# First layer of a two-layer trunk: products moved from GpSimd to VectorE, ScalarE and a load, gate weights folded in bulk, heads in another order

## The chip, the cores and the metric

One core of one Trainium2 chip runs the whole program in one launch. The metric is the device time of an execution in microseconds, here the median of three. Lower is better. Engines are named as in the profile: PE is TensorE, DVE is VectorE, ACT is ScalarE, POOL is GpSimd, SP is SyncE, which only issues transfers.

## The reference

The input x has 256 tokens of 1024 channels. The first layer is an mLSTM block, the second an attention block of three branches. The change touches the first layer alone, so here is what it computes:

```python
h = rmsnorm(x, ml_norm)
x_in, z = split(h @ w_in)                      # 2048 channels each
conv = sum(x_pad[:, tap:tap + S] * conv_w[tap] for tap in range(4))
x_conv = silu(conv + conv_b)
q, k = headwise(x_conv, w_q), headwise(x_conv, w_k)    # 4x4 blocks: 512 of them
v = headwise(x_in, w_v)
gates = concat([q, k, v]) @ w_if + b_if                # 8 gate rows, 4 heads
hh = mlstm(q * DH ** -0.5, k, v, i_pre, log_sigmoid(f_pre))
x = x + ((layernorm(hh) * ln_w + skip * x_conv) * silu(z)) @ w_out
```

## The kernel before, in words

Every large product is done in three: each weight is rounded to a high part and the remainder kept as a low part, the activations likewise, and high by high, low by high and high by low are summed. Weights come in units of 1 MB, each in two halves (load_unit, L258). SP loads a half into a raw buffer (L273; four of them, so two units), ACT rounds it (L274), and the remainder is made either by DVE (L280) or by ACT and a transfer that POOL issues and that adds in place (L277, L278). The units 0, 1, 2 and 11 have both remainders on DVE, most others have the second one by transfer.

The first layer begins with loads of x transposed, in four pieces, between the pieces of the unit 0. ACT and DVE make the high and low parts of x (L342, L343). The squares for the norm (L351 to L356) are two on POOL and two on ACT, their sums two on POOL and one on DVE. norm1 (L384) makes one row of 256 factors, rb1, with two small products on PE and a power on POOL (L325). It is called in the middle of the first evacuation.

A loop over four heads (L431) follows. Each head takes two units of the projection (project_channels, L402), and DVE multiplies each result by rb1 into the tile xin (L438, two buffers). In the first pass, after the first unit, SP is given the constants cst, the gate weights wif and x by tokens (L441 to L449), each kept back by a small DVE copy of a column of rb1. Then the head's products are prepared: POOL spreads the 4x4 blocks of two weights into block-diagonal tiles m (blockdiag, L396, with the mask bm out of cst), bdq for the query and key together, bdv for the value. DVE folds the gate weights of that head (gate_weights, L461, for bdv and for q). The convolution has four taps. The first is on ACT (L476), the others on DVE (L487, 44 in all), except that head 0 has its second tap on ACT (L480) and the sum on POOL (L482). ACT takes the SiLU of the whole head (L489). PE then makes q (L497), v (L504) and the scores (L511, L512). The tiles gva and gsc gather the gate columns (L508 on POOL, L516 on DVE).

After the heads, the value is split in high and low parts (split_v, L529): the low part is on POOL for the heads 0 and 2, on DVE for the heads 1 and 3. The gate chain, a second loop over heads (L591), eight units of z (L653) and the output projection (L694) follow. POOL multiplies x_conv by the skip weight, once per head (L641).

The program order is not the order on the engines. When the program is built, a planner walks through it in a simulation of time and puts each engine's instructions into a fixed order. An earlier line goes first where both could start, and a later line that is ready earlier may overtake. So the L641 products run among the heads, and the load of pkb, written at L724, is issued at the start. Each engine and each queue then keeps to its order: an instruction that waits holds all behind it.

Of the kernel before, what the change touches and what calls it, by code (L numbers as in the profile page):

```python
# [9 lines left out]
F32 = mybir.dt.float32  # L10
# [18 lines left out]
V_POOL = (0, 2)  # L29
# [106 lines left out]
def prep(x, ml_norm, ml_w_in, ml_conv_w, ml_conv_b, ml_w_q, ml_w_k, ml_w_v, ml_w_if, ml_b_if,  # L136
# [30 lines left out]
    wif = np.repeat(ml_w_if[0].reshape(3, 16, 32, 1, 4, 8), 4, 3).transpose(0, 2, 3, 1, 4, 5).reshape(3, P, 16, 4, 8)  # L167
    o["wif"] = np.concatenate([np.stack([wif[0], wif[1]], 2).reshape(P, 1024), wif[2].reshape(P, 512)], 1)
# [34 lines left out]
def trunk(ctx, tc, a, out, dbg=None):  # L203
# [80 lines left out]
    plan = [(a["wi1"], i, KT, 256) for i in range(16)] + [(a["wo1"], i, 4, 512) for i in range(8)]  # L284
# [44 lines left out]
    nc.sync.dma_start(pka, a["pka"])  # L329
# [54 lines left out]
    def norm1():  # L384
# [11 lines left out]
    def blockdiag(src, dt, n=P):  # L396
        t = T([P, 4, n], dt, tag="m2", bufs=M2)
# [33 lines left out]
    for h in range(NH):  # L431
        xin = T([P, 4, S + 3], tag="xin", bufs=2)
        GP.memset(xin[:, :, 0:3], 0.0)
        for u in range(2):
            def evac_x(ps, x_=xin[:, 2 * u:2 * u + 2, 3:], first=(h, u) == (0, 0)):
                if first:
                    norm1()
                V.tensor_tensor(x_, ps, spread(rb1), op=OP.mult)  # L438
            project_channels(a["wi1"], 2 * h + u, evac_x, ("px", "px", "acc1")[(2 * h + u) % 3])
            if (h, u) == (0, 0):  # L440
                V.tensor_copy(cst[:, 0:1], rb1[:, 0:1])  # L441
                nc.sync.dma_start(cst, a["cst"][:, 0:n_res])
                wifs = [T([P, 16, n // 128, 8], tag="zt", bufs=ZT, name="wif") for n in (1024, 512)]
                for t, o_, n in zip(wifs, (0, 1024), (1024, 512)):
                    V.tensor_copy(t[:, 0, 0, 0:1], rb1[:, 0:1])
                    nc.sync.dma_start(t.rearrange("p a b c -> p (a b c)"), a["wif"][:, o_:o_ + n])
                for i in range(2):
                    V.tensor_copy(xt[i][:, 0, 0:1], rb1[:, 0:1])
                    nc.sync.dma_start(xt[i], a["x"][:, i * 512:(i + 1) * 512].rearrange("(t p) c -> p t c", p=P))  # L449
# [694 lines left out]
```

## Time and profile before

| what | value |
|---|---|
| median of three runs | 377.86 us (377.17 to 378.06) |
| the profiled execution | 378.87 us |
| its span, first to last instruction | 377.1 us |
| mean granted TensorE clock | 0.984 |
| busy: PE, DVE, ACT, POOL | 350.6, 255.7, 241.5, 134.7 us |

The span is what the views of the trace are laid out on. The profiled execution is 1.77 us longer than its span, and 1.01 us longer than the median. A matmul's end is modelled, so a busy PE says that it had an instruction and not how fast it went; the granted clock says how fast.

### The profile page before, as it was taken

The page shows a single profiled execution, that of the slowest core. Times are in us where ns is not written, and L with a number is a line of the kernel's source. Part 1 is how long each engine was busy: PE and PEld are TensorE (multiplying, and loading weights), DVE is VectorE, ACT ScalarE, POOL GpSimd, SP SyncE. Part 2 cuts the span into 40 slices and gives each one's busy share as a digit, 9 for nine tenths or more (in the row PEclk, how much of TensorE's full clock was granted, in tenths as well). Part 3 has the DMA queues.
Part 4 walks back from the last instruction along what each step waited for, and adds up shares of the span by engine and source line. Part 5 has one row for each costly group of instructions (what it writes and reads, how often), then busy time and mean ns, then how long its engine had stood idle before and what let it go on. Part 6 is the DMA issues. An engine that isn't in the chain of part 4 may idle for free.

```text
span 377.1 us, 6621 instructions
## 1 busy us (share of the span) xinstructions
PE 350.6 (93%) x2399; PEld 313.8 (83%) x2399; DVE 255.7 (68%) x535; ACT 241.5 (64%) x438; POOL 134.7 (36%) x165
## 2 busy tenths in 40 slices
PE   6998799979999979999999799999879999999991
PEld 6998799869998968988887699999869996777771
DVE  5976999756476548983243736687979789684515
ACT  6674669738468649765653744372579789996304
POOL 5226377433301124610100303283430283857003
PEclk9999899999999999999999999999989999999997
DMA  7889758765646978999998897546577865020003
GB/s 260 280 269 315 209 129 217 188 152 125 167 157 159 197 210 217 228 233 296 239 262 239 266 343 216 173 104 155 154 195 209 246 237 158 2 56 2 2 0 112
DMA packets 21633, 69.57 MB, mean 185 GB/s; under 512 B 2528, under 2 KB 2912, under 8 KB 21600
## 3 DMA queue, kind: packets, MB, share of 16 engines
q1 hardware_dynamic: 15472, 48.71, 38.7%
q0 software_dynamic: 4752, 16.83, 24.6%
q10 hardware_dynamic: 1376, 3.61, 2.9%
q8 instruction: 19, 0.31, 0.3%
q14 instruction: 14, 0.11, 0.1%
HBM read 50.87 MB, written 1.05 MB: 138 GB/s over the span
## 4 chain that ended last, share of the span: by engine, by line
PE 39%; DMA 23%; DVE 18%; issue 8%; ACT 8%; POOL 1%; SPq 1%; ACTq 0%; POOLq 0%; DVEq 0%
PE ps L411 17%; DMA wl<-wr 7%; DMA wr<-in_wo_dram 6%; DVE xc L487 6%; PE ps L694 6%; DVE wl L280 4%; DMA wr<-in_wi2z_dram 3%; DMA wr<-in_wi2k_dram 2%; ACT wh L274 2%; PE ps L984 2%; PE ps L909 2%; PE ps L897 2%; DMA cst<-in_cst_dram 2%; DMA xch<-in_xt_dram 1%; ACT wl L277 1%
## 5 line engine op out<-in xcount | busy, mean ns | idle before, releaser
L411 PE MATMUL ps<-hT,wh 128*128 128x256 f32 x832 | 139.5, 293 | 2.4 <-DVE hT L343 1.3
L274 ACT ACTIVATE wh<-wr 128x1024 fp32r<-128x1024 f32 (+2 forms) x90 | 89.5, 1000 | 58.1 <-PE ps L411 21.5
L411 PEld LDWEIGHTS ps<-hT,wh 128*128 128x128 f32 x832 | 121.8, 198 | 4.6 <-DVE hT L343 1.9
L280 DVE TENSOR_TENSOR wl<-wr,wh 128x1024 fp32r<-128x1024 f32 (+2 forms) x57 | 70.9, 1244 | 36.0 <-ACT wh L274 33.2
L411 PE MATMUL ps<-hT,wl 128*128 128x256 f32 x416 | 87.7, 287 | 0.0
L411 PEld LDWEIGHTS ps<-hT,wl 128*128 128x128 f32 x416 | 66.4, 193 | 1.0 <-issue 0.6
L278 POOL DMA_DIRECT2D wl<-wr x33 | 28.7, 877 | 107.9 <-ACT wl L277 103.5
L277 ACT ACTIVATE wl<-wr 128x1024 fp32r<-128x1024 f32 (+1 forms) x33 | 33.8, 1025 | 13.4 <-PE ps L694 6.6
L694 PE MATMUL ps<-wh,r 128*128 128x512 f32 x128 | 41.4, 398 | 0.0
L487 DVE SCALAR_TENSOR_TENSOR xc<-xin,pka,xc 128x256 f32<-128x256 f32 x44 | 30.8, 754 | 0.1
L694 PEld LDWEIGHTS ps<-wh,r 128*128 128x128 f32 x128 | 24.0, 188 | 5.5
L694 PE MATMUL ps<-wl,r 128*128 128x512 f32 x64 | 25.3, 395 | 0.0
L694 PE MATMUL ps<-wh,y 128*128 128x512 f32 x64 | 21.8, 406 | 0.0
L803 POOL TENSOR_TENSOR swap<-swap,trig 128x512 f32<-128x512 f32 x6 | 10.2, 1697 | 18.9 <-DMA swap<-qu 7.3
L775 PE MATMUL ps<-wl,hT 128*128 128x280 f32 (+1 forms) x48 | 15.8, 330 | 1.2 <-DMA wl<-wr 1.2
L846 PE MATMUL ps<-ka,qt 128*128 128x256 f32 (+1 forms) x32 | 12.0, 380 | 3.8 <-DVE nm L852 3.7
L774 PE MATMUL ps<-wh,hT 128*128 128x280 f32 (+1 forms) x48 | 15.5, 329 | 0.0
L776 PE MATMUL ps<-wh,hT 128*128 128x280 f32 (+1 forms) x48 | 15.2, 325 | 0.0
L694 PEld LDWEIGHTS ps<-wh,y 128*128 128x128 f32 x64 | 11.8, 188 | 3.1 <-issue 0.8
L694 PEld LDWEIGHTS ps<-wl,r 128*128 128x128 f32 x64 | 12.0, 188 | 2.8 <-DMA wl<-wr 0.2
L641 POOL TENSOR_TENSOR xc<-xc,pka 128x1024 f32<-128x1024 f32 x4 | 9.8, 2455 | 12.2 <-PE ps L512 12.2
L504 PE MATMUL ps<-m,xin 128*128 128x136 f32 x64 | 9.7, 299 | 3.6 <-DVE m L464 3.5
(473 smaller groups left out, 676.0 us busy)
## 6 DMA issues: line engine op xcount, KB each, us to landing
wr<-in_wi_dram SPq DMA_DIRECT2D x34, 512.0 KB
wl<-wr POOLq DMA_DIRECT2D x31, 512.0 KB, 5.9
wr<-in_wo_dram SPq DMA_DIRECT2D x24, 512.0 KB
wr<-in_wi2k_dram SPq DMA_DIRECT2D x12, 512.0 KB
wr<-in_wi2z_dram SPq DMA_DIRECT2D x8, 512.0 KB
wr<-in_wi2v_dram SPq DMA_DIRECT2D x8, 280.0 KB
cw<-in_cw_dram ACTq DMA_DIRECT2D x4, 512.0 KB
xch<-in_xt_dram SPq DMA_DIRECT2D x4, 256.0 KB
```

The lines of the kernel that those rows point to most:

```text
L274: A.activation(hi[:, k, :], raw[:, k, :], AF.Copy)
L277: A.activation(lo[:, k, :], raw[:, k, :], AF.Copy, scale=-1.0)
L278: GP.dma_start(out=lo[:, k, :].rearrange("p k n -> p (k n)"), in_=raw[:, k, :].rearrange("p k n -> p (k n)"), accum_op=OP.add)
L280: V.tensor_tensor(lo[:, k, :], raw[:, k, :], f32(hi[:, k, :]), op=OP.subtract)
L411: PE.matmul(ps[:, c, :], w, (hl if i == 1 else hh)[:, k, :], start=(k, c, i) == (0, 0, 0), stop=(k, i) == (KT - 1, 2), skip_group_check=True)
L487: V.scalar_tensor_tensor(xc[:, c, :], xin[:, c, tap:tap + S], tap_w(tap, c), xc[:, c, :], op0=OP.mult, op1=OP.add)
L694: PE.matmul(acc, l, r[:, k % 2, cols], start=first and i == 0, stop=last and i == 2)
L774: PE.matmul(o_, lh, hi[:, k % 2, :], start=kt == 0, stop=False)
L775: PE.matmul(o_, lh, lo[:, k % 2, :], start=False, stop=False)
L776: PE.matmul(o_, ll, hi[:, k % 2, :], start=False, stop=kt == KT - 1)
L803: (GP, V)[RE[1]].tensor_tensor(sw, sw, turn(1), op=OP.mult)
L846: PE.matmul(o_, lq, ka[:, g, :, 0:w_], start=True, stop=False)
```

## The change

The squares are all on ACT and their sums on DVE. The high and low parts of x come ahead of the squares in program order, norm1 ahead of the projection, and the second unit's load behind norm1 (N0 is 1). The block-diagonal tiles of the value are loaded with their zeros (wvbd, 1.05 MB: 16 x 128 columns of 128 rows; in two loads, four columns of blocks and twelve). Those of the query are made on DVE. The gate weights of all heads are folded at once, those for the value ahead of head 0's convolution and those for the query behind it; POOL copies a head's part into q. Head 0's convolution becomes like the others'. The SiLU is taken by half a head. DVE takes the low parts of the values and the gva sums; two conversions (ident_r, maskt_r) go from DVE to POOL, and the halved factors rb1h from DVE to ACT. cst, wif and the first part of wvbd are kept back by a column of the squares instead of rb1, x by tokens and pkb by head 2's xin. The program order of projections (A) and products (B) of the heads becomes A0 A1 B0 A2 B1 A3 B2 B3.

```diff
-V_POOL = (0, 2)
-N0 = 2
-CA_ = (1, 2, 3)
-CB_ = (0,)
-CH = 1
+N0 = 1
 SQA = (2, 3)
-SQP = (1, 2)
+SQP = ()
+XTH = 2
+STAGES = "A0 A1 B0 A2 B1 A3 B2 B3"
...
+    o["wvbd"] = np.zeros((32, 4, 16, 32, 4), f)
+    o["wvbd"][np.arange(32), :, :, np.arange(32), :] = own(ml_w_v).reshape(32, 4, 16, 4)
+    o["wvbd"] = o["wvbd"].reshape(P, 16, P)
...
     ahead(N0)
-    nc.sync.dma_start(pka, a["pka"])
...
+    scaled(range(KT), lambda kt: xch0[kt // 4][:, kt % 4, :], gain1)
     sq1 = T([P, 4, S], tag="zt", bufs=ZT, name="sq1")
     for q in range(4):
...
-        (A.activation(o_, x_, AF.Square) if q in SQA else GP.tensor_tensor(o_, x_, x_, op=OP.mult))
+        A.activation(o_, x_, AF.Square)
         if q:
             (GP if q in SQP else V).tensor_tensor(sq1[:, 0:2, :], sq1[:, 0:2, :], o_, op=OP.add)
-    scaled(range(KT), lambda kt: xch0[kt // 4][:, kt % 4, :], gain1)
...
-        V.tensor_scalar(rb1h, rb1, 0.5, None, op0=OP.mult)
+        A.activation(rb1h, rb1, AF.Copy, scale=0.5)
+
+    norm1()
+    ahead(2)
+    nc.sync.dma_start(pka, a["pka"])
...
-        GP.tensor_tensor(t[:, :, 0:P].rearrange("p c (n j) -> p c n j", j=4),
-                         src[:, :, None, :].to_broadcast([P, 4, 32, 4]), bm, op=OP.mult)
+        V.tensor_tensor(t.rearrange("p c (n j) -> p c n j", j=4),
+                        src[:, :, None, :].to_broadcast([P, 4, 32, 4]), bm, op=OP.mult)
...
+    def heads_x(h):
+        xin = xins[h] = T([P, 4, S + 3], tag="xin", bufs=2)
+        GP.memset(xin[:, :, 0:3], 0.0)
+        for u in range(2):
+            def evac_x(ps, x_=xin[:, 2 * u:2 * u + 2, 3:]):
+                V.tensor_tensor(x_, ps, spread(rb1), op=OP.mult)
+            project_channels(a["wi1"], 2 * h + u, evac_x, ("px", "px", "acc1")[(2 * h + u) % 3])
+            if (h, u) == (0, 0):
+                small_weights()
+        if h == XTH:
+            V.tensor_copy(pkb[:, 0:1], xin[:, 0, 3:4])
+            nc.sync.dma_start(pkb, a["pkb"])
+            for i in range(2):
+                V.tensor_copy(xt[i][:, 0, 0:1], xin[:, 0, 3:4])
+                nc.sync.dma_start(xt[i], ...)
...
+    def small_weights():
+        bdvs = folded["bdv"] = T([P, 16, PG], name="bdv")
+        wifs = [T([P, 16, n // 128, 8], tag="zt", bufs=ZT, name="wif") for n in (1024, 512)]
+        V.tensor_copy(cst[:, 0:1], sq1[:, 0, 0:1])
+        nc.sync.dma_start(cst, a["cst"][:, 0:n_res])
+        for t, o_, n in list(zip(wifs, (0, 1024), (1024, 512)))[::-1]:
+            V.tensor_copy(t[:, 0, 0, 0:1], sq1[:, 0, 0:1])
+            nc.sync.dma_start(t.rearrange("p a b c -> p (a b c)"), a["wif"][:, o_:o_ + n])
+        for c, dep in ((slice(0, 4), sq1[:, 0, 0:1]), (slice(4, 16), rb1[:, 0:1])):
+            V.tensor_copy(bdvs[:, c.start, 0:1], dep)
+            nc.sync.dma_start(bdvs[:, c, 0:P], a["wvbd"][:, c, :])
...
+        def gate_weights(out, wgt, wif, nq):
+            tmp = T([P, 16, nq * 4, 8], tag="f4", bufs=F4, name="wtmp")
+            V.tensor_tensor(tmp, wif, wgt[:, :, :, None].to_broadcast([P, 16, nq * 4, 8]), op=OP.mult)
+            V.tensor_reduce(out, tmp.rearrange("p c i g -> p c g i"), axis=AX.X, op=OP.add)
+
+        gate_weights(folded["bdv"][:, :, P:PG], wv, wifs[1], 1)
+        gq = T([P, 16, 8], name="gwq")
+        folded.update(AT=AT, gq=gq, fold_q=lambda: gate_weights(gq, wqk, wifs[0], 2))
...
+            A.activation(xc[:, c, :], xin[:, c, 0:S], AF.Identity, scale=tap_w(0, c), bias=cbias)
         for c in range(4):
-            for tap in range(2 if h in CB_ else 1, 4):
+            for tap in range(1, 4):
                 V.scalar_tensor_tensor(xc[:, c, :], xin[:, c, tap:tap + S], tap_w(tap, c),
                                        xc[:, c, :], op0=OP.mult, op1=OP.add)
-        A.activation(xc, xc, AF.Silu)
+            if c % 2:
+                A.activation(xc[:, c - 1:c + 1, :], xc[:, c - 1:c + 1, :], AF.Silu)
+        if h == 0:
+            folded["fold_q"]()
...
-        gate_weights(q[:, :, S:SG], wqk, wifs[0], 2)
+        GP.tensor_copy(q[:, :, S:SG], folded["gq"][:, own, :])
...
-        GP.tensor_tensor(gva, gva, v[:, :, :, P:PG], op=OP.add)
+        V.tensor_tensor(gva, gva, v[:, :, :, P:PG], op=OP.add)
...
-    V.tensor_copy(ident_r, ident)
+    GP.tensor_copy(ident_r, ident)
-    V.tensor_copy(maskt_r, C("maskt")[:, None, :].to_broadcast([P, 2, P]))
+    GP.tensor_copy(maskt_r, C("maskt")[:, None, :].to_broadcast([P, 2, P]))
...
-        (GP if h in V_POOL else V).tensor_tensor(lo, src, f32(hi), op=OP.subtract)
+        V.tensor_tensor(lo, src, f32(hi), op=OP.subtract)
```

## Rows read from the trace of the kernel before

**Rows 1.** The page's busy times of the engines (busy us, share of the span, instructions).

```profile
PE 350.6 (93%) x2399; PEld 313.8 (83%) x2399; DVE 255.7 (68%) x535; ACT 241.5 (64%) x438; POOL 134.7 (36%) x165
```

**Rows 2.** Busy time of each engine in five stretches of the span: from:to in us, length, then busy us and instructions of PE, PEld, DVE, ACT and POOL, the granted TensorE clock, the share of the 16 DMA engines and GB/s.

```profile
11.80:36.50 24.70, 24.65 (x197) 24.45 (x197) 19.08 (x33) 15.04 (x20) 8.34 (x7) 1.00 0.87 277
36.50:40.90 4.40, 0.93 (x8) 0.96 (x9) 4.40 (x6) 0.00 (x0) 3.58 (x4) 1.00 0.58 216
40.90:44.40 3.50, 3.50 (x19) 3.50 (x19) 3.50 (x8) 3.24 (x6) 1.04 (x1) 0.53 1.02 219
...
77.00:79.50 2.50, 0.13 (x2) 0.00 (x0) 2.50 (x5) 0.00 (x0) 1.31 (x1) 1.00 0.98 211
...
139.50:200.00 60.50, 58.23 (x306) 49.09 (x307) 36.88 (x74) 42.71 (x55) 17.29 (x24) 1.00 0.94 241
```

**Rows 3.** What TensorE waited for in the first 160 us: waiting line, what released it, us in total, times, longest.

```profile
PE ps L504 <- DVE m L464: 3.5, 1, 3.5
PE ps L497 <- DVE gsc L516: 2.4, 1, 2.4
...
PE ps L411 <- DVE hT L343: 1.3, 2, 0.9
```

**Rows 4.** VectorE in order of time ahead of the first wait: start, us, line, operation, tiles and shapes, count, and in brackets the idle time before it with what ended it.

```profile
32.04 0.29 DVE L524 CAST maskt_r<-cst 128x256 fp32r<-128x256 f32 x1 [2.26 <-DMA cst<-in_cst_dram]
32.25 4.83 DVE L487 SCALAR_TENSOR_TENSOR xc<-xin,pka,xc 128x256 f32<-128x256 f32 x4
37.00 2.53 DVE L463 TENSOR_TENSOR wtmp<-wif,pka 128x128 f32<-128x128 f32 x2
```

**Rows 5.** GpSimd in the same time, the first and the last of its six tensor operations in a row from 32.15 to 39.26, with the columns of the group above.

```profile
32.15 1.09 POOL L398 TENSOR_TENSOR m<-AT,cst 128x512 f32<-128x512 f32 x1 [2.95 <-DMA cst<-in_cst_dram]
...
37.95 1.31 POOL L482 TENSOR_TENSOR xc<-xc,x 128x512 f32<-128x512 f32 x1
```

**Rows 6.** The chain of waits: start, us and what held the chain.

```profile
25.97 6.04 DMA cst<-in_cst_dram
```

**Rows 7.** VectorE around the second wait: one operation by itself; then, from other times with no GpSimd tensor operation beside them, six taps in a row and one remainder of a half unit.

```profile
73.40 5.20 DVE L487 SCALAR_TENSOR_TENSOR xc<-xin,pka,xc 128x256 f32<-128x256 f32 x1
...
60.53 2.45 DVE L487 SCALAR_TENSOR_TENSOR xc<-xin,pka,xc 128x256 f32<-128x256 f32 x6
...
26.70 1.22 DVE L280 TENSOR_TENSOR wl<-wr,wh 128x1024 fp32r<-128x1024 f32 x1
```

**Rows 8.** GpSimd at the time of that long operation.

```profile
73.78 2.20 POOL L641 TENSOR_TENSOR xc<-xc,pka 128x1024 f32<-128x1024 f32 x1
75.64 2.66 POOL L534 TENSOR_TENSOR vsp<-v,vsp 128x1024 fp32r<-128x1024 f32 x1
```

**Rows 9.** VectorE while the first unit starts, without and with GpSimd at work beside it.

```profile
5.61 0.87 DVE L343 SCALAR_TENSOR_TENSOR hT<-xch,pk,hT 128x256 fp32r<-128x256 f32 x2
6.41 1.52 DVE L280 TENSOR_TENSOR wl<-wr,wh 128x512 fp32r<-128x512 f32 x1
7.85 1.89 DVE L343 SCALAR_TENSOR_TENSOR hT<-xch,pk,hT 128x256 fp32r<-128x256 f32 x2
9.67 0.68 DVE L280 TENSOR_TENSOR wl<-wr,wh 128x512 fp32r<-128x512 f32 x1
```

**Rows 10.** GpSimd in that time, the last of the four operations on the squares.

```profile
9.81 1.69 POOL L356 TENSOR_TENSOR sq<-sq 128x512 f32<-128x512 f32 x1 [0.74 <-ACT sq L354]
```

**Rows 11.** VectorE from 20 to 105 us grouped by line and shape: line, operation, tiles, shapes, count | busy us, mean ns | idle before.

```profile
L438 DVE TENSOR_TENSOR xin<-ps,rb 128x512 f32<-128x512 f32 x8 | 5.5, 685 | 8.2 <-PE ps L411 8.2
...
L463 DVE TENSOR_TENSOR wtmp<-wif,pka 128x256 f32<-128x256 f32 x4 | 2.7, 680 | 0.0
L464 DVE TENSOR_REDUCE q<-wtmp 128x32 f32<-128x256 f32 x4 | 2.5, 628 | 0.0
L463 DVE TENSOR_TENSOR wtmp<-wif,pka 128x128 f32<-128x128 f32 x4 | 2.0, 495 | 0.0
L464 DVE TENSOR_REDUCE m<-wtmp 128x32 f32<-128x128 f32 x4 | 1.5, 372 | 0.0
```

**Rows 12.** GpSimd from 20 to 105 us, grouped in the same way.

```profile
L641 POOL TENSOR_TENSOR xc<-xc,pka 128x1024 f32<-128x1024 f32 x4 | 9.8, 2455 | 12.2 <-PE ps L512 12.2
...
L534 POOL TENSOR_TENSOR vsp<-v,vsp 128x1024 fp32r<-128x1024 f32 x2 | 6.0, 3010 | 0.0
L398 POOL TENSOR_TENSOR m<-pka,cst 128x512 f32<-128x512 f32 x4 | 4.8, 1210 | 2.9 <-DVE m L464 2.9
```

**Rows 13.** TensorE in order of time: the starts of two units one after the other.

```profile
28.88 2.32 PE L411 MATMUL ps<-hT,wh 128*128 128x256 f32 x18
...
34.64 1.84 PE L411 MATMUL ps<-hT,wh 128*128 128x256 f32 x14
```

**Rows 14.** ScalarE in order of time: the rounding of halves of the units 2 and 4, which needs their loads.

```profile
17.92 1.06 ACT L274 ACTIVATE wh<-wr 128x1024 fp32r<-128x1024 f32 x1 [1.66 <-DVE wl L280]
...
27.72 1.04 ACT L274 ACTIVATE wh<-wr 128x1024 fp32r<-128x1024 f32 x1
```

**Rows 15.** The DMA queues in the first 10 us (packets, MB, share of 16 engines): ScalarE's queue then carries only a load in rows of 544 bytes.

```profile
q10 hardware_dynamic: 144, 0.07, 2.9%
```

**Rows 16.** The chain of waits after the layer's heads: start, us, what held the chain.

```profile
167.58 5.79 DMA wl<-wr
...
173.43 3.77 DMA wr<-in_wo_dram
```

More of the change, by code (lines that the diff above doesn't have):

```diff
@@ L430, in trunk @@
     convw = CA("convw").rearrange("p (t c) -> p t c", t=4)
-    for h in range(NH):
-        xin = T([P, 4, S + 3], tag="xin", bufs=2)
+    xins, zt_ = {}, {}
+    def heads_x(h):
+        xin = xins[h] = T([P, 4, S + 3], tag="xin", bufs=2)
         GP.memset(xin[:, :, 0:3], 0.0)
         for u in range(2):
-            def evac_x(ps, x_=xin[:, 2 * u:2 * u + 2, 3:], first=(h, u) == (0, 0)):
-                if first:
-                    norm1()
+            def evac_x(ps, x_=xin[:, 2 * u:2 * u + 2, 3:]):
                 V.tensor_tensor(x_, ps, spread(rb1), op=OP.mult)
@@ L440, in trunk @@
             if (h, u) == (0, 0):
[L441 to L449, printed above, removed]
@@ new lines, in fold @@
+    def fold():
+        wifs = folded["wif"]
+        wqk = CA("wqk").rearrange("p (c i) -> p c i", c=16)
+        wv = CA("wv").rearrange("p (c i) -> p c i", c=16)
+        atmp = T([P, 16, 4, 4], tag="f4", bufs=F4, name="atmp")
+        V.tensor_tensor(atmp, CA("wkrep").rearrange("p (c i j) -> p c i j", c=16, i=4),
+                        wqk[:, :, 0:4, None].to_broadcast([P, 16, 4, 4]), op=OP.mult)
+        AT = T([P, 16, 4], name="AT")
+        V.tensor_reduce(AT, atmp.rearrange("p c i j -> p c j i"), axis=AX.X, op=OP.add)
+        def gate_weights(out, wgt, wif, nq):
[5 more added lines that the diff above has]
+        folded.update(AT=AT, gq=gq, fold_q=lambda: gate_weights(gq, wqk, wifs[0], 2))
@@ L469, in trunk, with heads_products @@
+    def heads_products(h):
+        if h == 0:
+            fold()
+        xin = xins.pop(h)
+        own = slice(4 * h, 4 * h + 4)
+        bdq = blockdiag(folded["AT"][:, own, :])
+        bdv = folded["bdv"][:, own, :]
         xc = T([P, 4, S], tag="f4", bufs=F4, name="xc")
         tap_w = lambda tap, c: convw[:, tap, 4 * h + c:4 * h + c + 1]
-        if h in CB_:
-            x1 = T([P, 4, S], tag=XT, bufs={"zt": ZT, "sc2": 1}[XT], name="x1")
         for c in range(4):
             cbias = CA("convb")[:, 4 * h + c:4 * h + c + 1]
-            if h in CA_ or h in CB_:
-                A.activation(xc[:, c, :], xin[:, c, 0:S], AF.Identity, scale=tap_w(0, c), bias=cbias)
-            else:
-                V.tensor_scalar(xc[:, c, :], xin[:, c, 0:S], tap_w(0, c), cbias, op0=OP.mult, op1=OP.add)
-            if h in CB_:
-                A.activation(x1[:, c, :], xin[:, c, 1:1 + S], AF.Copy, scale=tap_w(1, c))
-                if CH and c % 2:
-                    GP.tensor_tensor(xc[:, c - 1:c + 1, :], xc[:, c - 1:c + 1, :], x1[:, c - 1:c + 1, :], op=OP.add)
@@ L519, in trunk, with silu_z1, evac_z @@
         scs.append(sc)
+    def silu_z1(h):
+        z = zt_[h] = T([P, 4, S], name="z")
+        for u in range(2):
+            def evac_z(ps, z=z[:, 2 * u:2 * u + 2, :]):
+                V.tensor_tensor(z, ps, spread(rb1), op=OP.mult)
+                A.activation(z, z, AF.Silu)
+            project_channels(a["wi1"], 8 + 2 * h + u, evac_z)
+    for stage in STAGES.split():
+        {"A": heads_x, "B": heads_products, "Z": silu_z1}[stage[0]](int(stage[1]))
     ident_r = TS([P, P], F32R, name="ident_r")
-    V.tensor_copy(ident_r, ident)
+    GP.tensor_copy(ident_r, ident)
     maskt_r = T([P, 2, P], F32R, name="maskt_r")
-    V.tensor_copy(maskt_r, C("maskt")[:, None, :].to_broadcast([P, 2, P]))
+    GP.tensor_copy(maskt_r, C("maskt")[:, None, :].to_broadcast([P, 2, P]))
     causal = C("mask2")
@@ L646, in trunk @@
     for h in range(NH):
-        z = T([P, 4, S], tag="zt", bufs=ZT, name="z")
-        for u in range(2):
+        z = zt_[h] if h in zt_ else T([P, 4, S], tag="zt", bufs=ZT, name="z")
+        for u in range(0 if h in zt_ else 2):
             def evac_z(ps, z=z[:, 2 * u:2 * u + 2, :]):
@@ L722, in after_block @@
         squares(ss2, n, tb)
-    nc.sync.dma_start(pkb, a["pkb"])
     gain2 = CB("g")
```

26 lines of the change are left out of this document (7 added, 19 removed).

## The prediction

> **What bounds the kernel now.** I read the busy times first, then a table by stretch, then TensorE's waits, then the queues of the engine that each wait names. TensorE is busy for 350.6 of 377.1 us [rows 1], so a change is worth what it takes out of TensorE's idle time or of its time at the lower clock. In the stretch 11.8 to 36.5 it is full: 24.65 of 24.70 us at a granted clock of 1.00 [rows 2]. Then come 4.40 us with only 0.93 us of work, and 3.50 us at 0.53, which is the lower level of 1.2 GHz; it fell after the idle time [rows 2]. The wait is for the gate columns of the value's block-diagonal tile, DVE's L464, 3.5 us [rows 3]. A second hole is at 77.0 to 79.5, 2.4 us for gsc [rows 2, 3].
>
> Both waits name DVE, and both come from POOL beside it. Six taps in a row take 2.45 us, 0.41 each, with no tensor operation on POOL [rows 7]; four ahead of the first wait take 4.83, 1.2 each, and two small products 2.53 [rows 4], while POOL works without a pause [rows 5]. In the second case one tap lasts 5.20 us [rows 7], and POOL's L641 and L534 fill 73.78 to 78.30 [rows 8]. The gsc addition stands behind that tap. Ahead of the first wait there is also a load: cst needs 6.04 us from its issue at 25.97 [rows 6], and DVE's queue stood 2.26 us for it at maskt_r [rows 4].
>
> **The change part by part.**
>
> *First wait.* The cause of the slowing goes: five block-diagonal products and one addition of taps leave POOL [rows 5]. maskt_r leaves DVE's queue, and cst is let go by a column of the squares, not of rb1. Gain 3.5 us of idle time [rows 3] and half of the 3.50 us at half clock [rows 2], 1.75: together 5.2. Bounds: nothing (DVE is still late, below) to 5.2.
>
> *Second wait.* L534 leaves POOL, but L641 stays, which the diff doesn't touch: four, 9.8 us [rows 12]. Without the 2.66 us of L534 [rows 8] the long tap ends 2.66 earlier, more than the 2.4 of the wait. Gain 2.4, bounds 0 to 2.4.
>
> *The start.* POOL's squares and sums slow DVE here too: a pair of L343 takes 0.87 alone and 1.89 beside POOL, a quarter unit's remainder 0.68 and 1.52 [rows 9, 10]. TensorE waits 1.3 us for L343 [rows 3]. Those operations go. Against it, ACT gets two more squares; a square isn't among my rows, so I price one by DVE's 0.68 for the same 128x512 [rows 9]. They stand behind the parts of x in program order. I take 1.0 us of gain, near the 1.3 that is waited for; bounds 2.0 (two slowed pairs give 1.0 each) to a loss of 1.4 (both squares in the path).
>
> *What DVE takes on before head 0's products.* From 11.8 to 36.5 it is busy 19.08 us [rows 2]. Off: 4 x 0.8 for the taps' slowing, 3.2; maskt_r and rb1h, 0.29 each at the row of the former [rows 4], 0.6. On: two sums of squares 1.4 and one block-diagonal product 0.7 by the 0.68; eight more taps 3.3; the value's gate weights for four heads at once, 4 x (0.50 + 0.37) = 3.5 by the slowed means [rows 11]. That makes 24.2 of 24.7 us. It fits, with nothing over. Their cover is the first four units on TensorE, and the fifth, which can run without head 0. The query's fold, 4 x (0.68 + 0.63) = 5.2 [rows 11], comes behind the taps, where it delays DVE but not TensorE's value products. The price if the cover is short is a new wait; I put 1.0 us for all such waits, bounds 0 and 5.2, the first wait over again.
>
> *A later head.* DVE: two remainders 1.22 each [rows 7], two evacuations 0.69 each [rows 11], twelve taps 4.9, a block-diagonal product 0.7, the value's low part 1.22 by the same row, small sums under 0.5: 11.1, and up to 2.45 more where L641 holds it [rows 12]. TensorE needs two units of 5.76 (28.88 to 34.64 [rows 13]), 11.5, and the head's own products. So DVE, which held TensorE up, is then covered. ACT loses the four second taps of head 0 and gets rb1h and half-head SiLUs: no term, since no wait of TensorE in the layer but at the start names it.
>
> *Loads.* wvbd adds 1.05 MB. In its rows of 512 bytes I estimate 4.4 us, from a load in rows of 544: 0.07 MB for 2.9% of 10 us [rows 15]. x by tokens, 1.05 MB, leaves the stretch before 36.5 for head 2, so that stretch (0.87 busy) carries the same bytes. The SP queue now has cst, wif and a quarter of wvbd, 1.3 MB, near 15 us instead of 26. At 277 GB/s [rows 2] this sets weights behind it back by 4.7 us. Unit 2's second half is rounded by 18.98 and needed at 23.1; unit 4's by 28.76 and needed at 34.64 [rows 13, 14]: margins of 4.1 and 5.9. I put 0, bounds 0 to 0.6. The other three quarters wait for rb1, with the loads of unit 3 and later behind them on SP. x and pkb wait for head 2's xin; behind them stand only units from 8 on.
>
> The trace has 6.04 us for a load of 228 KB [rows 6], far more than its bytes. The Trainium skill (DMA: Bandwidth & Descriptors, Queues, rings and completion order) says that SP owns one ring on each of the DMA engines and that its descriptors are consumed in ring order; by that rule the weights take their turn behind the small loads, and the trace agrees with it for cst behind weights. With this rule the 4.7 us falls on the unit 2 in full and the sum is 0.6 worse; without it, nothing is added.
>
> *On POOL's queue,* ident_r, maskt_r (waiting for cst) and the copies of q's gates (waiting for the fold) now stand ahead of transfers that make remainders. No wait of TensorE in the layer's rows names such a transfer [rows 3], so they get no term of their own; the allowance of 1.0 holds it.
>
> **Sum.** 378.87 - 5.2 - 2.4 - 1.0 + 1.0 = 371.3 for an execution like the profiled one, which is 1.0 above the median. So 370.3.
>
> **The rivals.**
>
> *POOL isn't done.* The change says that GpSimd only issues transfers, but L641 stays, and the power. One L641 alone is 2.45 on average [rows 12], and if it meets the tap ahead of gsc again, the second wait stays: 372.7. Against it speaks the 2.66 above. Chance 0.12.
>
> *The wait moves to the bulk fold.* DVE's 24.2 of 24.7 leaves no room; a load of wif that is 5 us late puts head 0's value products as late as before. The wait and the low clock stay, 5.2, and 378.87 - 2.4 - 1.0 - 1.0 + 1.0 gives 375.5 as a median. For it: L464 is what TensorE waits for now, and its work is now four heads' at once. Against it: cst and wif come sooner, and unit 4 can go first. Chance 0.10.
>
> *Given back later.* From 160 us the chain of waits goes through loads and in-place transfers by turns [rows 16], with the DMA engines at 0.94 [rows 2]. If they set the pace there, the gain becomes a wait for weights: 377.9. Against it: in that stretch TensorE has 58.23 of 60.50 us of work [rows 2], and raw buffers come free by its pace. Chance 0.07.
>
> *Slower: SP held for rb1 ahead of unit 3.* rb1 was there just before cst's issue at 25.97 [rows 6]. It now needs two more squares on ACT and two more sums on DVE, 2.7 by the 0.68. If SP stands until 28.7, then 0.79 MB of wvbd and 1.05 MB of unit 3 need 6.6 us at 277 GB/s, and a rounding 1.06: 36.4. TensorE wants unit 3 at 27.9 (28.88 less 1.0), waits 8.5 us and runs at half clock behind it, 1.75: 370.3 + 10.2 = 380.5. It outweighs the gain once rb1 comes after about 26. Against it: norm1 is now ahead of the projection in program order, so its small products needn't queue behind a unit. Chance 0.09. By the ring rule that I cited this would be at its worst.
>
> **How the numbers follow.** The forecast has 0.62. 0.3% of 377.9, 1.1 us, is about what a measurement of this kernel can tell from no change. Faster: 0.62 + 0.12 + 0.10 = 0.84. No difference: 0.06, most of the third rival. Slower: 0.10. The low end is all gains with 2.0 at the start and no new wait, 368.3, less the 2.3 us that TensorE stands idle between 139.5 and 200 [rows 2], should the heads' chain come sooner: 366.0. The high end takes in the second rival: 375.5. About 0.2 lies outside.
>
> **What would show it.** Right: no wait of TensorE over 1 us between 12 and 100 us, the granted clock at 1.00 throughout that stretch, taps at 0.41 except beside L641, L504 of head 0 before 36, the first unit running on from about 10.8. Wrong on the fold: a wait for an L464-like reduction in head 0. Wrong on loads: ACT's rounding waiting for weights between 20 and 36 and TensorE after it. Wrong later: waits for weights after 160 us that grow by what the layer gained. The forecast fails if TensorE still has over 3 us of idle time between 12 and 100 us.

## The result, and the profile after

The change makes the kernel slower: 382.31 us (median of 4 runs, 381.79 to 383.82) against 377.96 (377.17 to 378.12), a ratio of 1.0126 with the interval [1.0092, 1.0159]. Predicted were 370.3. In the experiments below the medians leave out two single executions, of 672 us in e3 and 563 us in e6, and the ratios compare the executions in the chip's faster state alone.

The profiled execution after took 383.82 us, with a span of 382.0. Its busy times, which answer to [rows 1]:

```profile
PE 355.6 (93%) x2399; PEld 315.4 (83%) x2399; DVE 249.7 (65%) x539; ACT 242.6 (63%) x441; POOL 111.0 (29%) x151
```

GpSimd lost 23.7 us of work, VectorE 6.0. TensorE runs the same 2399 instructions and is busy for 5.0 us longer. The stretches, in the columns of [rows 2]:

```profile
11.80:28.60 16.80, 16.80 (x135) 16.65 (x133) 14.20 (x26) 9.32 (x11) 3.51 (x3) 1.00 0.92 320
28.60:31.40 2.80, 0.11 (x2) 0.08 (x1) 2.80 (x6) 2.08 (x3) 0.00 (x0) 0.87 1.07 249
31.40:37.50 6.10, 6.10 (x29) 6.10 (x30) 6.10 (x8) 4.32 (x7) 1.21 (x3) 0.50 1.00 268
37.50:100.00 62.50, 62.50 (x475) 60.53 (x475) 41.05 (x78) 45.01 (x72) 16.41 (x18) 1.00 0.72 200
...
150.50:203.00 52.50, 49.05 (x212) 38.20 (x211) 19.98 (x25) 28.16 (x34) 6.86 (x8) 1.00 0.94 248
```

Both old waits are gone: from 37.5 to 100 us TensorE has no idle time at all. But a new hole stands at 28.6 us, with 6.1 us at half clock behind it, where before it was 3.50. TensorE's waits of over 1 us in the first 160 us, in the columns of [rows 3]:

```profile
PE ps L417 <- ACT wl L281: 2.7, 1, 2.7
PE ps L417 <- ACT wh L278: 2.1, 2, 1.9
```

The second lies in the first unit, before 14 us. The first is the new hole, and it is misnamed: the ScalarE instruction that ended last belongs to unit 4. The product that waits is unit 3's first, and unit 3 needs the part of PSUM, the memory into which TensorE writes its sums, that unit 0's evacuation (L444, VectorE's copy out of it) frees. e5 below bears this out: with that evacuation early, unit 3 starts at 28.70, while the same ScalarE instruction ends at 31.37. VectorE's queue shows where that evacuation was, in the columns of [rows 4]:

```profile
23.36 0.48 DVE L380 TENSOR_SCALAR dg<-pk,r 128x128 f32<-128x128 f32 x2 [0.60 <-POOL r L329]
24.49 3.08 DVE L404 TENSOR_TENSOR m<-AT,cst 128x512 f32<-128x512 f32 x4 [0.65 <-DMA cst<-in_cst_dram]
27.49 0.68 DVE L484 TENSOR_TENSOR wtmp<-wif,pka 128x512 f32<-128x512 f32 x1
28.09 1.21 DVE L284 TENSOR_TENSOR wl<-wr,wh 128x1024 fp32r<-128x1024 f32 x1
29.23 0.41 DVE L392 COPY rb<-ps 128x256 f32<-128x256 f32 x1
...
30.52 0.68 DVE L444 TENSOR_TENSOR xin<-ps,rb 128x512 f32<-128x512 f32 x1
```

All four heads' block-diagonal products, a wait for cst, the fold's first product and unit 4's remainder stand ahead of rb1's copy. The planner queued what it took to be ready first.

The taps show that what the prediction blamed is nearly cured. They took 754 ns on average before (first line) and take 510 now, one of them 2.11 us beside an L674. The operations of [rows 7] and [rows 12], from 20 to 105 us:

```profile
L487 DVE SCALAR_TENSOR_TENSOR xc<-xin,pka,xc 128x256 f32<-128x256 f32 x44 | 30.8, 754 | 0.1
```

```profile
L505 DVE SCALAR_TENSOR_TENSOR xc<-xin,pka,xc 128x256 f32<-128x256 f32 x48 | 21.9, 510 | 1.8 <-ACT xc L502 1.8
...
L674 POOL TENSOR_TENSOR xc<-xc,pka 128x1024 f32<-128x1024 f32 x4 | 8.8, 2206 | 18.8 <-PE ps L533 18.8
```

**Where the time went.** A few times of TensorE in each kernel's profile, in us (worked out from its rows): the end of head 3's scores, the first and the last product of the output projection, the last small product of the second layer's norm, the last product of all, and the difference of the last two.

```
kernel                  scores   projection        norm 2   last    layer 2
before                  100.98   156.91  203.56    213.57   369.43  155.86
after                    95.73   150.45  201.27    210.15   374.28  164.13
e1_new_old2              94.15   148.87  198.72    206.67   364.11  157.44
e2_old_new2             102.91   156.31  203.44    210.78   377.38  166.60
e4_no_inplace            95.30   149.15  199.78    206.41   362.36  155.95
e5_dve_again             92.32   147.04  196.49    205.08   363.68  158.60
e6_both                  95.62   149.46  198.07    206.39   364.24  157.85
e7_one_line              96.73   153.97  204.71    213.72   382.30  168.58
e8_queues_old            92.66   147.38  196.91    205.30   387.62  182.32
e9_no_inplace_wo1        93.96   147.80  195.31    201.95   357.38  155.43
e10_no_inplace_rb1       91.54   145.38  192.90    199.54   355.72  156.18
e11_bdq_gpsimd           96.53   151.25  201.20    210.03   368.72  158.69
e12_old_no_inplace      100.71   154.63  201.37    208.00   364.64  156.64
```

The changed kernel is 6.46 us ahead when the projection begins, loses 4.17 of them inside it, gains 1.13 up to the norm, and loses 8.27 in the second layer, whose code the diff doesn't touch: -6.46 + 4.17 - 1.13 + 8.27 = 4.85, the distance of the two last products. The second layer before and after, in the columns of [rows 2]:

```profile
213.57:369.43 155.86, 151.99 (x1114) 133.27 (x1112) 108.79 (x282) 97.93 (x229) 61.41 (x77) 0.99 0.50 142
```

```profile
210.15:374.28 164.13, 156.90 (x1114) 134.05 (x1112) 112.46 (x282) 98.08 (x230) 62.21 (x76) 0.98 0.47 136
```

Of the 8.27 us, 3.36 are idle time of TensorE. In the other 4.91 it is busy for longer with the same 1114 products.

### The profile page after: what moved, and what is told of

Same layout as the page of the kernel before. It is cut to its first block, busy times and chain, and to the rows that moved or that the text cites. A ratio compares the mean times of both kernels' runs of the same rounds, so it can differ in the third digit from the quotient of the medians.

```text
span 382.0 us, 6618 instructions
## 1 busy us (share of the span) xinstructions
PE 355.6 (93%) x2399; PEld 315.4 (83%) x2399; DVE 249.7 (65%) x539; ACT 242.6 (63%) x441; POOL 111.0 (29%) x151
## 3 DMA queue, kind: packets, MB, share of 16 engines
HBM read 51.92 MB, written 1.05 MB: 139 GB/s over the span
## 4 chain that ended last, share of the span: by engine, by line
PE 66%; DMA 14%; DVE 10%; issue 5%; ACT 3%; POOL 0%; ACTq 0%; POOLq 0%; SPq 0%; DVEq 0%
PE ps L417 30%; PE ps L727 8%; DMA wl<-wr 7%; DMA wr<-in_wo_dram 4%; DVE wl L284 2%; PE ps L941 2%; PE ps L648 2%; PE ps L929 2%; PE ps L525 2%; PE ps L1016 2%; PE ps L532 2%; PE ps L518 2%; PE ps L807 2%; PE ps L878 2%; DMA xch<-in_xt_dram 1%
## 5 line engine op out<-in xcount | busy, mean ns | idle before, releaser
L284 DVE TENSOR_TENSOR wl<-wr,wh 128x1024 fp32r<-128x1024 f32 (+2 forms) x57 | 70.0, 1229 | 36.4 <-ACT wh L278 34.1
L417 PE MATMUL ps<-hT,wl 128*128 128x256 f32 x416 | 89.5, 289 | 0.0
L417 PEld LDWEIGHTS ps<-hT,wl 128*128 128x128 f32 x416 | 67.3, 194 | 2.5 <-issue 2.1
L281 ACT ACTIVATE wl<-wr 128x1024 fp32r<-128x1024 f32 (+1 forms) x33 | 33.9, 1026 | 11.8 <-DMA wr<-in_wo_dram 6.4
L505 DVE SCALAR_TENSOR_TENSOR xc<-xin,pka,xc 128x256 f32<-128x256 f32 x48 | 21.9, 510 | 1.8 <-ACT xc L502 1.8
L807 PE MATMUL ps<-wl,hT 128*128 128x280 f32 (+1 forms) x48 | 16.8, 350 | 1.1 <-DMA wl<-wr 1.1
L806 PE MATMUL ps<-wh,hT 128*128 128x280 f32 (+1 forms) x48 | 16.0, 344 | 0.4 <-ACT wh L278 0.4
L808 PE MATMUL ps<-wh,hT 128*128 128x280 f32 (+1 forms) x48 | 16.0, 342 | 0.0
L674 POOL TENSOR_TENSOR xc<-xc,pka 128x1024 f32<-128x1024 f32 x4 | 8.8, 2206 | 18.8 <-PE ps L533 18.8
L835 POOL TENSOR_TENSOR swap<-swap,trig 128x512 f32<-128x512 f32 x6 | 9.3, 1553 | 14.8 <-DMA swap<-kraw 13.0
L444 DVE TENSOR_TENSOR xin<-ps,rb 128x512 f32<-128x512 f32 x8 | 5.4, 686 | 12.5 <-PE ps L417 12.5
```

The costliest lines, as they stand in the source:

```text
L281: A.activation(lo[:, k, :], raw[:, k, :], AF.Copy, scale=-1.0)
L284: V.tensor_tensor(lo[:, k, :], raw[:, k, :], f32(hi[:, k, :]), op=OP.subtract)
L417: PE.matmul(ps[:, c, :], w, (hl if i == 1 else hh)[:, k, :], start=(k, c, i) == (0, 0, 0), stop=(k, i) == (KT - 1, 2), skip_group_check=True)
L505: V.scalar_tensor_tensor(xc[:, c, :], xin[:, c, tap:tap + S], tap_w(tap, c), xc[:, c, :], op0=OP.mult, op1=OP.add)
L806: PE.matmul(o_, lh, hi[:, k % 2, :], start=kt == 0, stop=False)
L807: PE.matmul(o_, lh, lo[:, k % 2, :], start=False, stop=False)
```

## The experiments

The second layer's code is the same in both kernels, and the order lists of e1 and e2 hold the same 1591 instructions of it, but the planner queued them otherwise: on TensorE 268 of 1036 stand at the same place, on VectorE 45 of 228. So an order can be moved from one kernel to the other, by edges that fix only the order of issue.

**e1, the changed kernel with the old order in the second layer.**

```
+def in_order(tc, first):       # at the end of trunk; first: the trace's length after layer[0].close()
+    ins = tc.nc.cur_bb.bb.instructions[first:]
+    info = _mb.DependencyInfo(_mb.DependencyClass.NoSync, _mb.DependencyReason.DATA)   # issue order only
+    for places in L2_ORDER.values():          # one list of places for each engine
+        for a, b in zip(places, places[1:]):
+            tc.add_manual_dep(ins[b], ins[a].name, info, reason="in_order")
```

> The changed kernel; every engine's queue of the first layer is as it was, and the second layer's instructions, whose code the change doesn't touch, are queued on each engine in the order that they had before the change. Theory 'order': the changed kernel is 3.3 us ahead of the old one when the second layer's projections begin (about 228 us) and loses some 8 us between 264 and 308 us because the planner queued the second layer in another order; with the old order it keeps the lead: 374 to 375.5 us, and the z units start about 3 us earlier than in the kernel before. Rival 'state': what the first layer leaves behind (loads that lie otherwise, VectorE's work that piled up) costs it, whatever the order: 380 to 382.5 us.

Measured: 373.86 us (372.82 to 374.42), 0.989 [0.980, 0.998] of before. The second layer takes 157.44 us, 1.58 more than before and 6.69 less than in the changed kernel.

**e2, the kernel before with the new order in the second layer** (the same edit with the other lists).

> The kernel before; its first layer as it was, its second layer in the order that the changed kernel has. Theory 'order': 378.0 + 8 = 384 to 387 us, with the z units late. Rival 'state': within 1.5 us of the kernel before, 377 to 379.5 us.

Measured: 389.38 us (386.13 to 391.90), 1.032 [1.014, 1.050]; second layer 166.60. The swap works in both directions, so 'order' stands and 'state' falls: the order alone costs the second layer as much as the change lost there, or more (10.74 us here). Both times lie just outside the bounds that 'order' gave, e1 below and e2 above.

**e7, one line of the change in the kernel before.**

```
-        V.tensor_scalar(rb1h, rb1, 0.5, None, op0=OP.mult)
+        A.activation(rb1h, rb1, AF.Copy, scale=0.5)
```

> The kernel before with one line of the change alone: rb1h is scaled on ScalarE (0.4 us) and no longer on VectorE. Nothing waits for it before 100 us, so by the work it is worth 0 to 0.5 us. The planner however orders the second layer nearly as in the changed kernel then (its sync queue instruction for instruction, 804 of 1036 places of TensorE the same, against 267 that are as before). Theory 'order': 383 to 388 us, most of it lost after 264 us. Rival 'state': 377 to 379 us.

Measured: 391.86 us (388.10 to 393.94), 1.030 [1.023, 1.037]. One instruction of 0.4 us moved between engines costs 12 us of median here (380.07 before on that chip). Its waits of 0.9 us and more from 215 us on, then the changed kernel's, then those of e1 (columns of [rows 3]):

```profile
PE ps L846 <- DVE nm L852: 2.8, 1, 2.8
PE ps L1007 <- DVE kcb L1001: 1.3, 1, 1.3
PE ps L411 <- DVE z L929: 1.2, 1, 1.2
PE ps L775 <- DMA wl<-wr: 0.9, 1, 0.9
```

```profile
PE ps L878 <- DVE nm L884: 2.8, 1, 2.8
PE ps L1039 <- DVE kcb L1033: 1.3, 1, 1.3
PE ps L417 <- DVE z L961: 1.2, 1, 1.2
PE ps L807 <- DMA wl<-wr: 1.1, 1, 1.1
```

```profile
PE ps L879 <- DVE nm L885: 3.7, 2, 2.6
PE ps L1017 <- issue: 0.9, 1, 0.9
```

Two kernels with different first layers share a list of waits, and they share most of an order (804 of TensorE's 1036 places, as the expectation says). e2, which has the new order whole, has the same four: 2.8, 1.7, 1.2 and 0.8 us. Where the waits are, the granted clock is lower too: the 46 us in which the scores run, in the changed kernel and in e1 (columns of [rows 2]):

```profile
264.00:310.00 46.00, 40.06 (x281) 35.18 (x279) 36.91 (x100) 35.01 (x85) 17.75 (x24) 0.93 0.68 198
```

```profile
260.00:306.00 46.00, 42.27 (x325) 40.53 (x325) 37.58 (x88) 35.13 (x80) 19.75 (x22) 0.96 0.70 208
```

In the new order 281 products are done in that time, in the old 325.

**e8, only SyncE's and GpSimd's queues in the old order** (their two lists of e1, the other three of the changed kernel).

> The changed kernel; in the second layer TensorE, VectorE and ScalarE keep the order that they have there, SyncE's and GpSimd's queues get the old one (the loads of the z units behind the swaps of q1, the swaps' products ahead of the values' block-diagonal ones). If the order of these two queues is what costs (swaps late, so q1's keys and scores late): 374 to 376.5 us. If it is the order of the three other engines (z units' matmuls and the scores' exponentials): 381 to 383.5 us.

Measured: 399.23 us, 1.053 [1.046, 1.059], worse than either whole order. Both expectations miss. The mixture is an order of its own and doesn't tell what either part of it costs; which move costs most stays open.

**e3 and e5, rb1 ahead in VectorE's queue.** Every queue is held as in e1, with one stretch of VectorE's changed:

```
-[m h0, m h1, m h2, m h3, wtmp, wl unit 4, rb1, reduce, xin u0, bdv column, xin u1, xin u2]
+[wl unit 4, rb1, xin u0, bdv column, xin u1, m h0, wtmp, reduce, xin u2, m h1, m h2, m h3]
```

> e1_new_old2 with one move in VectorE's queue and every other queue held as it is there: the copy of rb1 and the evacuations of units 0 and 1 go ahead of the four block-diagonal products and the fold's first product. Theory 'queue': PE's 2.7 us wait at 28.7 us is for the evacuation that stands behind these; it goes, the second half of the half-clock stretch (6.8 us, before the change 3.4) goes with it, 2.7 + 1.7 = 4.4 us at 38 us, and 2 to 4.4 us at the end against e1_new_old2. Rival 'norm': the squares' small products stand behind unit 1 on PE and rb1 is late anyway; the wait shrinks by under 1 us and the end moves by under 0.5 us. Third: what is gained at 38 us is given back at 160 to 205 us in waits for loads: under 1 us at the end.

> The program of e3_dve_move once more: the execution whose profile was kept there took 672 us with TensorE slow from end to end and can't be read, and its three others (371.6 to 375.0 us) don't differ from e1_new_old2 (372.8 to 374.4 us). Theory 'queue': PE's wait at unit 3 (1.9 to 2.9 us at 28.4 us) is gone in the profile, and 371 to 372 us. Theory 'given back': the wait is gone there, and PE waits by as much more for loads and low parts between 160 and 205 us: 373 to 374.5 us. Rival 'norm': the wait stands, under 1 us less.

Measured: e3 373.34 us (371.63 to 375.02), 0.988 [0.975, 1.001]; e5 374.74 us (370.25 to 378.84), 0.980 [0.972, 0.988], on another chip. VectorE in e5:

```profile
26.39 0.42 DVE L392 COPY rb<-ps 128x256 f32<-128x256 f32 x1 [0.34 <-PE ps L381]
26.85 0.69 DVE L444 TENSOR_TENSOR xin<-ps,rb 128x512 f32<-128x512 f32 x1
```

rb1 is 2.84 us earlier than in the changed kernel, unit 3 starts at 28.70 (there 31.35, in e1 30.98) without a wait. So 'queue' holds for the wait and 'norm' falls. Of the lead over e1, 1.83 us as the projection begins, 1.59 are left at the second layer's norm and 0.43 at the last products, and the totals don't tell the two kernels apart. So 'given back' has the end right and the place wrong: most of it goes in the second layer, and not in waits for loads between 160 and 205 us.

**e4, e9 and e12, fewer adding transfers.** e4 sets one constant; e9 also takes units 16 to 23 out; e12 does e9's edit in the kernel before. All hold the old second layer and leave the first to the planner.

```
-BOTH = (15, 16, 17)
+BOTH = ()
```
```
-BY_DMA = [... if i not in NOT_POOL] + ...
+BY_DMA = [... if i not in NOT_POOL and not 16 <= i < 24] + ...
```

> e1_new_old2, but the first halves of units 15 to 17 get their low parts from VectorE as their neighbours do, not by an adding transfer that GpSimd issues. Theory 'transfers': from 160 to 205 us the changed kernel loses 4 us of its lead in PE's waits for these units' low parts and loads; three transfers of 512 KB less on the queues give back 1.5 to 3 us against e1_new_old2. Rival 'loads': the raw loads themselves set the pace there, PE waits as long for wr: within 0.5 us. Rival 'VectorE': its three more subtractions of 1.22 us delay the heads: slower by 0.5 to 2 us.

> e4_no_inplace, and units 16 to 23, the first layer's output projection, get all their low parts from VectorE: no adding transfer is issued for them, eight of 512 KB less between 140 and 200 us, and eight subtractions of 1.22 us more on VectorE, which is busy 3 to 6 of each 10 us there. Theory 'engines full': the sixteen transfer engines are 97 to 103% busy from 150 to 200 us in all of these kernels, and adding transfers hold them as long as raw loads of nearly twice the bytes; so the lead over the old kernel at the end of the projection, 6.5 to 7.2 us whatever it was at 160 us, grows to 8.5 to 10 us: 368.5 to 370.5 us. Rival 'loads': raw loads alone fill the stretch and PE waits for them as long: within 0.7 us of e4's 371.7 us. Rival 'VectorE': its low parts come late for PE: 372 to 374 us.

> The kernel before, with the transfers of e9_no_inplace_wo1 taken out: units 15 to 17 and 16 to 23 get their low parts from VectorE; the second layer's order is held. It tells whether the full transfer engines already cost the old kernel time, or only what arrives 7 us earlier than it. The old kernel's projection shows no wait for these low parts (its rows: 128 products by 'wh' and 64 by 'wl' with 0.0 idle), but two waits of 1.4 and 1.8 us follow at 206 and 211 us as the second layer begins. Theory 'only when early': those two waits shrink by what the loads gain, and nothing else moves: 375 to 377 us. If the transfers held the old kernel as much as the changed one: 371 to 374 us. If VectorE's eleven subtractions come late behind its backlog of the heads: 378 to 381 us.

Measured: e4 371.72 us (370.94 to 372.75), 0.984 [0.975, 0.993]; e9 368.71 (367.06 to 369.77), 0.975 [0.968, 0.981]; e12 375.17 (372.86 to 378.25), 0.994 [0.990, 0.998]. TensorE's waits of the changed kernel from 150 to 225 us, and its stretch from 150 to 200 us with its DMA queues there (packets, MB, share of the 16 engines; q0 carries the adding transfers, q1 SyncE's):

```profile
PE ps L727 <- DMA wl<-wr: 3.0, 3, 1.5
PE ps L381 <- ACT wh L278: 2.2, 1, 2.2
PE ps L727 <- DVE x L749: 0.5, 1, 0.5
```

```profile
150.00:200.00 50.00, 46.55 (x204) 36.24 (x203) 18.77 (x24) 27.60 (x34) 6.86 (x8) 1.00 0.95 249
```

```profile
q0 software_dynamic: 1263, 4.58, 48.5%
q1 hardware_dynamic: 2156, 7.86, 46.2%
```

The same of e9, in which no wait is listed from 150 to 225 us:

```profile
150.00:200.00 50.00, 49.94 (x220) 39.85 (x219) 34.55 (x41) 26.24 (x34) 2.94 (x5) 1.00 0.60 191
```

```profile
q1 hardware_dynamic: 2448, 8.92, 53.6%
q0 software_dynamic: 144, 0.52, 5.5%
```

The transfer engines were busy for 95% of the stretch, a little less than the 97 to 103% of the expectation, and half of their time went to 4.58 MB of adding transfers. Without them TensorE's projection takes 47.5 us instead of 50.8, and the norm follows 6.64 us after it instead of 8.88. The table bears it out: the kernels that keep all these transfers and begin the projection between 147.0 and 154.0 us (the changed one, e1, e5, e7, e8, e11) need 49.45 to 50.82 us for it; the kernel before and e2, which begin after 156, need 46.65 and 47.13; e9 and e10, without the transfers, 47.5, though they begin by 147.8. The time is the one that 'engines full' gave, and VectorE had room: 18.77 us of work became 34.55.

How the transfers cost this isn't settled. SyncE's queue in the changed kernel, from 140 to 205 us, stands for them too (columns of [rows 3]):

```profile
SPq L277 <- DMA wl<-wr: 43.7, 11, 10.2
```

A load waits there until an adding transfer has read the raw buffer that it is to fill. e9 takes away most of this wait (6.8 us are left) together with the traffic, so full engines and held buffers aren't told apart. The kernel before had both, 43.5 us of this wait and a DMA share of 0.97 from 150 to 200 us, while TensorE never paused there.

e4 alone gains 2.1 us on e1, the size that 'transfers' gave, but not in its place: at the second layer's norm it is 0.26 us ahead of e1 in the two profiles, the rest comes after it, and TensorE still waits 2.0 us in the projection for low parts that come by transfer. e12 shows that the kernel before paid too. From the first product of the projection to the norm it takes 53.37 us instead of 56.66, and its two waits there, 2.8 us in all, are gone from the list; e9 against e1 gains 3.65 in the same part. Its time is in the 375 to 377 of 'only when early', but that it paid less than the changed kernel isn't shown: the projection also begins 2.28 us earlier, and that expectation had nothing else move.

The Trainium skill (DMA: Bandwidth & Descriptors, Issuing engines are not separate DMA queues) says that transfers of all issuing engines run on the same 16 DMA engines and interleave; the trace agrees, 48.5% and 46.2% from two queues filling one set.

**e6 and e10, both remedies.** e6 is e4 with e3's move. e10 is e9, with the move left to the planner by two edges of issue order:

```
+        with tc.issue_after(rows_at[h]):      # rows_at[h]: the evacuation of head h's second unit
+            V.tensor_tensor(t.rearrange(...), src..., bm, op=OP.mult)
...
+        with tc.issue_after(rows_at[0]):
+            gate_weights(folded["bdv"][:, :, P:PG], wv, wifs[1], 1)
```

> e4_no_inplace with the same move in VectorE's queue, every other queue as e4_no_inplace has it: the changed kernel with the old order of the second layer, low parts of units 15 to 17 on VectorE, and rb1 ahead of the block-diagonal products. If the loads no longer take back what is gained at 38 us: e4's 371.7 less 2 to 4 us = 368 to 369.7 us, the time that was predicted for the change or a little below. If they still do: 371 to 372 us.

> e9_no_inplace_wo1, with head h's block-diagonal product queued on VectorE behind the evacuation of that head's second unit and the fold's gate products behind that of head 0's. Theory 'engines full': the 2.8 us that this takes out of the unit 3 wait at 28 us (measured in e5_dve_again) now reaches the end: 366 to 368.5 us. If the lead is still taken back by 205 us: the time of e9_no_inplace_wo1 within 0.7 us.

Measured: e6 371.60 us (369.09 to 377.13), 0.976 [0.970, 0.982]; its profile has lost the unit 3 wait and got one of 3.4 us for ScalarE's evacuation of q at 50 us, in an order that was made for other times. So it decides nothing between its two expectations. e10: 365.71 us (365.37 to 367.72), 0.968 [0.963, 0.973], the fastest kernel here, 3.2% faster than before; e9 ran on the same chip at 368.71. Its hole at 28.6 us is filled (columns of [rows 2]):

```profile
28.60:31.40 2.80, 2.80 (x26) 2.80 (x25) 2.80 (x6) 2.32 (x3) 0.17 (x1) 1.00 1.05 269
31.40:37.50 6.10, 6.10 (x54) 6.10 (x53) 6.10 (x9) 4.16 (x6) 3.05 (x4) 1.00 1.09 297
```

In the 6.1 us that ran at half clock, 54 matmuls instead of 29 are done. With the transfers gone, the gain of the first layer comes through the projection whole: e10 is ahead of e9 by 2.42 us as the projection begins, 2.41 at the norm, 1.66 at the last products and 3.0 by the medians.

**e11, the four block-diagonal products back on GpSimd**, in e1 (the planner orders the first layer anew).

```
-        V.tensor_tensor(t.rearrange("p c (n j) -> p c n j", j=4),
+        GP.tensor_tensor(t.rearrange("p c (n j) -> p c n j", j=4),
```

> e1_new_old2 with the four block-diagonal products for the scores back on GpSimd: one part of the change undone. Theory 'shared': a VectorE instruction that meets such a product lasts until it ends, as in the kernel before (5.20 us for a tap of 0.41); four products of about 2.3 us from 25 us on hold rb1's copy, the evacuations and the first taps: VectorE takes 4 to 8 us more there than the 3.1 us that it is spared, and PE's wait at unit 3 grows from 2 to 4 to 7 us; 374 to 378 us at the end, less what the loads take back anyway. Rival 'spared': VectorE is spared 3.1 us ahead of rb1, the unit 3 wait goes, the time is 371.5 to 373.5 us.

Measured: 376.47 us (372.65 to 379.29), 0.995 [0.990, 0.999]; e1 was 0.989. VectorE and GpSimd at 25 us, and TensorE's wait at unit 3, 4.9 us, where e1 has 1.8:

```profile
25.16 4.55 DVE L484 TENSOR_TENSOR wtmp<-wif,pka 128x512 f32<-128x512 f32 x1 [1.68 <-DMA wif<-in_wif_dram]
```

```profile
24.77 4.38 POOL L404 TENSOR_TENSOR m<-AT,cst 128x512 f32<-128x512 f32 x4
```

```profile
PE ps L417 <- DVE bdv L468: 4.9, 1, 4.9
```

One VectorE product that takes 0.68 us in the changed kernel's row lasts 4.55, while GpSimd's four run. 'Shared' holds, at a smaller size: VectorE is held once, 3.9 us, and its taps up to 60 us came later and met nothing (487 ns on average). The Trainium skill (SBUF — State Buffer, Who interferes with whom) says that a VectorE instruction with two SBUF inputs contends with a GpSimd instruction that reads SBUF. The trace agrees, 4.55 us beside 4.38: the product was held through all four of GpSimd's, and not through the first alone.

## Why the prediction was wrong

- *First wait, second wait* (-5.2, -2.4): right in cause. Both waits are gone from the list, taps last 0.51 us on average, and e11 brings a hold back by putting products on GpSimd. The rival *POOL isn't done* didn't come true: the one tap that L674 held made no product of TensorE wait. "No wait of TensorE over 1 us between 12 and 100 us" failed all the same, through the next point, and head 0's value products, expected before 36, start at 39.88 us. The sign for a failed forecast, over 3 us of idle time there, didn't show (2.69), although the forecast failed.
- *What DVE takes on before head 0's products* (24.2 of 24.7 us, with 1.0 for new waits): this step failed first. It added up VectorE's busy time but not the order in its queue. It counted one block-diagonal product, 0.7; four, 3.08 us, stood ahead of rb1, with the load of cst ahead of them. The price was 2.7 us of idle time and half of 6.1 us, 5.8 in all, a little over its bound of 5.2; in e5, without the wait, unit 4 starts 4.33 us earlier. The rival *The wait moves to the bulk fold* had the mechanism, a VectorE queue without room, with the wrong victim: not head 0's value products but unit 3's PSUM bank.
- *Slower: SP held for rb1* didn't happen as put. rb1 came at 29.23, past the 26 that was named as the point, but unit 3 didn't wait for weights; it waited for rb1 itself through the evacuation. What spoke against it, that norm1 "needn't queue behind a unit", was wrong: program order isn't queue order, and its small products ran at 25.54 in the middle of unit 2.
- *The start* (-1.0): no gain is shown. The 49th of the units' products starts at 16.11 us instead of 16.50, but at 16.67 in e1, whose first layer is queued alike. The wait for L343 is gone. But a square stands ahead of the first rounding in ScalarE's queue, although it stands behind in program order, and the first product starts at 7.08 us instead of 6.18 (columns of [rows 4]):

```profile
5.89 0.61 ACT L358 ACTIVATE sq<-xch 128x512 f32<-128x512 f32 x1
6.41 0.61 ACT L278 ACTIVATE wh<-wr 128x512 fp32r<-128x512 f32 x1
```

- *Loads* (0) and the rival *Given back later* (0.07): mis-sized, 0 where 4.17 were lost. Early, 0 was right: TensorE has no wait for weights from 11.8 to 28.6 us, so the 0.6 that the ring rule would add didn't show. But the 4.17 us lost between 150 and 201 us are that rival, in part, and e9 shows that the adding transfers cause it. [Rows 16] and the DMA share of 0.94 in [rows 2] had pointed to it. The argument against it, that TensorE had work for 58.23 of 60.50 us there, says only that loads kept up with the old pace; it doesn't say that they had anything to spare.
- *The sum* let the second layer stand as it was: a term at nothing without a reason, and this one turned the sign. No step priced it, and no rival did. The runs put 8.27 us there (e1: 1.6 of them left), from an order that the planner made anew for the whole program. The sum's lead of 7.6 us was 6.46 as the projection began, 3.42 at the second layer's norm, and a loss of 4.85 at the last product. With the old order the change gives 373.86 us, inside the range of 366.0 to 375.5 and 3.6 above the forecast. e10, without the unit 3 wait and the transfers, is at 365.71, 8.2 below e1: more than the 3.6, since the transfers cost the kernel before as well.
- *A gain outside the sum.* A wait of the kernel before at 139.5 us, of which the prediction took account only in its low end, is gone too:

```profile
PE ps L615 <- ACT hn L639: 2.3, 1, 2.3
```

So the forecast's direction was right for the part that was argued and its sign was lost to one that wasn't. Its 6.46 us as the projection began are near 7.6 partly by luck: a price of 5.8 that was put at 1.0 met gains that stood outside the sum, like the 2.3 us above. Settled are the new wait's place (e5, e10), the cost of the transfers (e9, e12) and that of the order (e1, e2, e7). Open are how the transfers cost it, why the second layer's products are busy for 4.91 us longer, and which instruction of the new order costs what: the lists of the engines can be mixed in few ways, and the one that ran, e8, told nothing of it.

## What to carry to other kernels

Where a planner orders the whole program, a change anywhere can re-order everything behind it: compare the queues of the untouched part first, and hold them by edges of issue order before a change is judged, or a good change is thrown away for a bad order. When work moves to an engine, write down its queue and not its sum: ask what stands behind the new work, and tie new work that nobody waits for behind what others wait for. A stretch whose transfer engines are 95% busy may have nothing to give to a TensorE that arrives earlier, as here, even where it shows no wait at the old pace; look there first for where a gain will be given back.

## What the runs showed of the hardware

An adding transfer within SBUF holds the transfer engines longer than a load: in the changed kernel from 150 to 200 us 4.58 MB took 48.5% of the sixteen engines and 7.86 MB of loads 46.2%, 5.3 us for each MB against 2.9. In e9, where the engines are busy for 0.60 of that time, it is 5.3 against 3.0 (0.52 MB for 5.5%, 8.92 MB for 53.6%), so the price isn't one of full engines alone. After 2.7 us of idle time the granted clock stood at 0.50 (1.2 GHz) for all 6.10 us of a stretch in which TensorE never paused; after the 3.5 us wait before the change it was 0.53 over 3.50 us [rows 2].
